# A trunk kernel whose weight sum of gate and up is formed by VectorE instead of an accumulating load

## The chip, the cores and the metric

The kernel runs on one core of one Trainium2 chip. The metric is the device time of one execution in microseconds (us). TensorE multiplies matrices, VectorE and ScalarE work on tiles element by element, GpSimd and SyncE (SP) mainly issue transfers (DMAs). Each engine takes its own instructions in order; semaphores hold an instruction back until what it needs is there.

## What is computed

A trunk of two layers on x of 512 tokens by 1024, in float32. In each layer, a SwiGLU block comes before and after a mixing block:

```python
def swiglu(h, w_gate, w_up, w_down):
    return (jax.nn.silu(h @ w_gate) * (h @ w_up)) @ w_down

for l in range(DEPTH):
    x = x + 0.5 * swiglu(rms_norm(x, ffn1_norm[l]), ffn1_wg[l], ffn1_wu[l], ffn1_wd[l])
    ...
    x = x + 0.5 * swiglu(rms_norm(x, ffn2_norm[l]), ffn2_wg[l], ffn2_wu[l], ffn2_wd[l])
return rms_norm(x, final_norm)
```

The gate and up weights `wg` and `wu` are 1024 by 2816, so there are four such blocks (FFNs) with 11 column blocks of 256. The change concerns only how a sum of raw weights is formed for the products with `wg` and `wu`.

## The kernel before, in words

*Precision.* TensorE multiplies in a reduced format. Each operand is therefore split into a high part (a cast on ScalarE) and a low part (raw minus high, on VectorE), both at line 228, and three products are taken: high x high, high x low and low x high. The weights' parts are the tiles `wh` and `wl`, three buffers each; those of the activations are called by their form, for example `fb11h` and `fb11l`.

*Stages.* An FFN walks over its column blocks in the order of `INNER` (line 33; the last FFN uses `LAST`): one plain block, then `("w", b)` stages for b = 1, 3, 5, 7, 9, each of which handles a pair of gate and up for two column blocks. A `w` stage uses a scheme with seven products in place of eight. Its seven weight forms, in the order of `FORMS` (line 38), are built from raw quarters of `wg` and `wu`. With g0, g1 for the upper and lower half of the 1024 rows of `wg` and u0, u1 for `wu`:

- a11 = g0
- a12 = g1
- s2 = g0 + u0 + u1
- s3 = u0 + g0
- s1 = u0 + u1
- a22 = u1
- s4 = a12 + s2

Each form comes in two halves, h0 and h1, of two 128-row chunks each, so a stage has fourteen halves. For each, `stream` (line 831) runs 12 matmuls of 128 x 512. `winograd2` (line 985) runs the stage on TensorE by `CHAINS` (line 69): a11 into x, a12 into w, s2 into x, s3 into y, s1 into x, a22 into y, s4 into x. For each half it first calls `take_split`, which makes the raw tiles and splits two halves ahead, and it then combines the accumulators x, y, w on VectorE and ScalarE (lines 1011 to 1029): L1014 adds for the gates, L1022 and L1025 subtract, L1026 and L1029 multiply with the gates.

*Raw tiles and queues.* `seven` (line 375) enters ten raw units per stage in this order: a11, s1, a12, s3, a22, two halves each. Units s1 and s3 name two sources each. `need_raw` (line 212) gives a unit one of eight raw buffers and issues its plain load on SP's queue (`load`, line 207, L210). A second source is added by an accumulating load on GpSimd's queue (L223), which waits until the first load has landed. `need_split` (line 236) makes the forms: before s2 is split, VectorE adds s1 to a11 in place (L269), and after s3 VectorE adds that sum to a12 in place (L291), which is s4. A raw buffer is free again when the last split of its tile is done; the next unit in line then takes it.

*Order.* A scheduler sets the order of instructions on each engine at build time, by dependencies; it may move a VectorE instruction well ahead of its place in the text. Once built, the order is fixed.

The first layer's first FFN is called with `near=True` and treats b = 1 and b = 3 specially; the stages b = 9 go over into the next kind of stage (`share`, line 846), which reads `wd` and is not touched.

Of the kernel before, what the change touches and what calls it, by code (L numbers as in the profile page):

```python
# [75 lines left out]
def trunk_kernel(  # L76
# [23 lines left out]
    nc = tc.nc  # L100
# [92 lines left out]
    units = []  # L193
# [6 lines left out]
    def add_unit(*unit):  # L200
        units.append(unit)
        return len(units) - 1
# [24 lines left out]
    def split(hi, lo, raw, eng=nc.vector):  # L227
        return nc.scalar.copy(hi, raw), eng.tensor_sub(lo, raw, f32(hi))  # L228

    def split_far(hi, lo, raw):  # L230

        nc.scalar.activation(lo, raw, AF.Copy, scale=-1.0)
        nc.scalar.copy(hi, raw)
        return nc.gpsimd.dma_start(out=f32(lo), in_=raw, accum_op=ALU.add)

    def need_split(g):
        while state["split"] <= min(g, len(order) - 1):
            n = state["split"]
            u, what = order[n]
            far = what == "far"  # L240
            if what in (None, "far"):
                need_raw(u if far else max(u, min(u + LOAD_AHEAD, state["hold"] or len(units))))
                raw = raw_of.pop(u)
            elif isinstance(what, tuple) and what[0] == "end":

                _, what, h = what
                at = {"a11": 2, "s2": 2, "s3": 3, "s1": 3, "a12": 4, "a22": 5, "s4": 5}[what]
                need_raw(u + 3 * at + h + LOAD_AHEAD)
                raws = {name: u + 3 * i + h for i, name in enumerate(END_LOADS)}
                if what == "s2":  # L250
                    with tc.issue_after(state["rest"]):
                        nc.vector.tensor_add(raw_of[raws["a11"]], raw_of[raws["a11"]], raw_of[raws["s1"]])
                raw = raw_of[raws["a11" if what in ("s2", "s4") else what]]
            elif isinstance(what, tuple):

                what, h, how = what
                far = how == "far"
                last = {"a11": 0, "a12": 4, "s2": 2, "s3": 6, "s1": 2, "a22": 8, "s4": 4}[what]
                need_raw(u + h if far else u + max(last, 4) + h + LOAD_AHEAD)
                a11, s1, a12, s3, a22 = (raw_of.get(u + 2 * i + h) for i in range(5))  # L260
                if what == "s2":

                    late = state["late"] if h else None
                    if not state["late"] and how == "share":
                        late = state["rest"]
                    if how == "behind":
                        late = state["mark"]
                    with tc.issue_after(late) if late else nullcontext():
                        nc.vector.tensor_add(a11, a11, s1)  # L269
                raw = {"a11": a11, "a12": a12, "s2": a11, "s3": s3, "s1": s1, "a22": a22, "s4": a12}[what]  # L270
            shape = list(raw.shape)
            hi = wpool.tile(shape, F32R, tag="wh", bufs=3, name=f"wh_{n}")
            lo = wpool.tile(shape, F32R, tag="wl", bufs=3, name=f"wl_{n}")
            if far:
                sent = split_far(hi, lo, raw)
            else:
                state["cast"], state["rest"] = (i.ins for i in split(hi, lo, raw))
                if isinstance(order[n][1], tuple) and order[n][1][2] == "mark":
                    state["mark"] = state["rest"]
            if isinstance(order[n][1], tuple) and order[n][1][0] == "end":  # L280
                if what == "a12":
                    nc.gpsimd.dma_start(out=raw_of[raws["a11"]], in_=raw, accum_op=ALU.add)
                if what in ("s3", "s1", "a12", "a22"):
                    del raw_of[raws[what]]
                if what == "s4":
                    del raw_of[raws["a11"]]
            elif isinstance(order[n][1], tuple):
                if what == "s3" and how == "share":
                    nc.gpsimd.dma_start(out=a12, in_=a11, accum_op=ALU.add)
                elif what == "s3":  # L290
                    nc.vector.tensor_add(a12, a12, a11)  # L291
                done = {"s3": (0, 3), "s1": (1,), "a22": (4,), "s4": (2,)}.get(what, ())
                for i in done:
                    del raw_of[u + 2 * i + h]
            split_of[n] = (hi, lo)
            state["split"] += 1
            if far:

                with tc.issue_after(sent.ins):
                    need_raw(u + LOAD_AHEAD + (4 + h if isinstance(order[n][1], tuple) else 0))  # L300
# [26 lines left out]
    def abreast(kc):  # L327

        return max(1, KC // kc) if kc in (2, 4) else 1
# [34 lines left out]
    def plan():  # L364
        def cols(src, k0, kc, n, how=None, last=False):
            wide = abreast(kc)
            for b in halves_of(n, wide, last):
                order.append((add_unit((src, k0, kc, b * P, wide * P)), how))

        def plain(wg, wu, b):  # L370
            for w in (wg, wu):
                for j in range(2):
                    order.append((add_unit((w, 0, KC, (2 * b + j) * P, P)), None))

        def seven(at, how):


            u = len(units)
            for what in (((0, 0),), ((1, 0), (1, 1)), ((0, 1),), ((1, 0), (0, 0)), ((1, 1),)):
                for h in range(2):  # L380
                    add_unit(*(at(o, j, h) for o, j in what))
            order.extend((u, (what, h, how(what, h))) for what in FORMS for h in range(2))

        def ffn(wg, wu, wd, stages, near=False):
            for what, b in stages:
                how = "far" if b == (0,) and not near else None
                if what == "p":
                    plain(wg, wu, b)
                if what == "w":
                    seven(  # L390
                        lambda o, j, h: ((wg, wu)[o], KC // 2 * j + 2 * h, 2, 2 * b * P, S),
                        lambda what, h: "far"
                        if (b, what, h) == (1, "a11", 0)
                        else {("a12", 0): "mark", ("s2", 1): "behind"}.get((what, h))
                        if near and b == 3
                        else None,
                    )
                if what == "s":
                    seven(
                        lambda o, j, h: (wd, 2 * b + KC // 2 * j + 2 * h, 2, o * S, S),  # L400
                        lambda what, h: "share",
                    )
                if what == "d":
                    cols(wd, 2 * b[0], 2 * len(b), KC, how, len(b) == 2)
                    if len(b) == 2:
                        closing.append(len(units) - 1)
                if what == "e":
                    u = len(units)
                    roomy.update(range(u, u + 3))
                    for form_ in END_LOADS:  # L410
                        ojs = {"s1": ((1, 0), (1, 1)), "s3": ((1, 0), (0, 0))}
                        for i in range(3):
                            add_unit(
                                *(
                                    (wd, 2 * b + (KC + 2 * j if i == 2 else KC // 2 * j + 2 * i), 2, o * S, S)
                                    for o, j in ojs.get(form_, ((0, int(form_ == "a12")) if form_ != "a22" else (1, 1),))
                                )
                            )
                    order.extend((u, ("end", what, i)) for what in END_FORMS for i in range(3))

        for l in range(DEPTH):
            ffn(ffn1_wg[l], ffn1_wu[l], ffn1_wd[l], INNER, l == 0)
            for c in MIX_COLS:
                for j in range(2):
                    order.append((add_unit((w_in[l], 0, KC, (2 * c + j) * P, P)), None))
            seven(
                lambda o, j, h: (w_out[l], KC // 2 * j + 2 * h, 2, o * S, S),
                lambda what, h: "share",
            )
            ffn(ffn2_wg[l], ffn2_wu[l], ffn2_wd[l], INNER if l + 1 < DEPTH else LAST)  # L430
# [1349 lines left out]
```

## Time and profile before

| | |
|---|---|
| median of 3 runs | 1625.92 us (1625.47 to 1626.92) |
| the profiled execution's own time | 1628.27 us |
| its span, first to last instruction | 1626.5 us |
| TensorE busy | 1616.2 us |
| VectorE busy | 1367.3 us |
| ScalarE busy | 1177.8 us |
| GpSimd busy | 223.5 us |
| mean data rate of the DMAs | 196 GB/s |
| accumulating loads of `wg` on GpSimd's queue | 40, of 512 KB each |

In the profile PE is TensorE's matmuls, PEld its weight loads, DVE is VectorE, ACT ScalarE, POOL GpSimd, and SPq the queue of SyncE. L228 is line 228. A row of a timeline gives start and duration in us from the span's start, engine, line, operation, output tile <- input tiles, the shape, how many instructions were merged into the row, and in brackets the idle time of the engine before it with what ended it. A DMA's row shows its issue; its landing, when the data has arrived, is given apart.

### The profile page before, as it was taken

To read this page: it belongs to the slowest core of one execution; us is meant where nothing else is said; L and a number is where in the kernel's file an instruction comes from. 1 tells how busy PE (TensorE), PEld (TensorE's weight loads), DVE (VectorE), ACT (ScalarE), POOL (GpSimd) and SP (SyncE) were. 2 spreads that over 40 slices of the span, in tenths; PEclk is the share of its full clock that TensorE was granted. 3 is DMA by queue.
4 is the path that set the end of the run, shared out by engine and by line. 5 is a ranking of instruction groups with operands and counts; after the bars stand their busy time and mean duration, and the time that the engine had idled before them with its cause. 6 is when DMAs were issued, how large, how long until landed. Compare 5 with 4: busy or idle time off the path is not lost.

```text
span 1626.5 us, 21177 instructions
## 1 busy us (share of the span) xinstructions
PE 1616.2 (99%) x7571; PEld 1349.5 (83%) x7571; DVE 1367.3 (84%) x1780; ACT 1177.8 (72%) x1511; POOL 223.5 (14%) x199
## 2 busy tenths in 40 slices
PE   9999999999999999999999999999999999999998
PEld 7888888888898878888888888888888988888887
DVE  7978797988899877797999777989788998677997
ACT  6677777857766577778865777788586767878665
POOL 1211111001211111111011111110012111111121
PEclk9999999999999999999999999999999999999999
DMA  9999999912597798999867899999136978999992
GB/s 269 213 231 213 215 215 236 242 58 77 145 230 170 177 218 214 214 218 246 224 147 186 215 216 221 211 245 224 48 91 154 235 149 215 228 221 226 231 264 71
DMA packets 307182, 318.12 MB, mean 196 GB/s; under 512 B 125628, under 2 KB 188676, under 8 KB 307076
## 3 DMA queue, kind: packets, MB, share of 16 engines
q1 hardware_dynamic: 265412, 230.90, 49.6%
q0 software_dynamic: 41200, 85.47, 30.7%
q8 instruction: 59, 0.97, 0.2%
q14 instruction: 47, 0.39, 0.1%
q10 hardware_dynamic: 464, 0.40, 0.1%
HBM read 264.29 MB, written 2.10 MB: 164 GB/s over the span
## 4 chain that ended last, share of the span: by engine, by line
PE 96%; DMA 2%; DVE 1%; ACT 0%; issue 0%; SPq 0%; POOL 0%; DVEq 0%; POOLq 0%
PE x L837 26%; PE y L837 13%; PE x_s L837 9%; PE acc L318 7%; PE acc L319 7%; PE acc L321 7%; PE w L837 7%; PE y_s L837 4%; PE x_m L822 3%; PE w_s L837 3%; PE y_m L822 1%; DMA raw<-in_ffn_wu_dram 1%; PE y_e L837 1%; PE x_e L837 1%; PE acc L699 1%; PE w_m L822 1%
## 5 line engine op out<-in xcount | busy, mean ns | idle before, releaser
L228 DVE TENSOR_TENSOR wl<-raw,wh 128x1024 fp32r<-128x1024 f32 (+1 forms) x494 | 598.7, 1219 | 171.4 <-ACT wh L228 170.3
L228 ACT CAST wh<-raw 128x1024 fp32r<-128x1024 f32 (+1 forms) x494 | 513.8, 1043 | 304.7 <-PE x L837 92.9
L318 PE MATMUL acc<-xh,wh 128*128 128x512 f32 x392 | 153.3, 393 | 0.5 <-ACT wh L228 0.5
L319 PE MATMUL acc<-xl,wh 128*128 128x512 f32 x392 | 153.1, 391 | 0.0
L321 PE MATMUL acc<-xh,wl 128*128 128x512 f32 x384 | 149.6, 390 | 0.0
L223 POOL DMA_DIRECT2D raw<-in_ffn_wu_dram x40 | 50.3, 1268 | 384.3 <-DMA raw<-in_ffn_wu_dram 182.6
L318 PEld LDWEIGHTS acc<-xh,wh 128*128 128x128 f32 x392 | 73.8, 188 | 15.1 <-ACT wh L228 0.6
L319 PEld LDWEIGHTS acc<-xl,wh 128*128 128x128 f32 x392 | 73.7, 188 | 14.4
L321 PEld LDWEIGHTS acc<-xh,wl 128*128 128x128 f32 x384 | 72.1, 188 | 15.2
L223 POOL DMA_DIRECT2D raw<-in_ffn_wg_dram x40 | 49.4, 1248 | 201.8 <-DMA raw<-in_ffn_wu_dram 92.0
L223 POOL DMA_DIRECT2D raw<-in_ffn_wd_dram x34 | 41.1, 1216 | 248.8 <-DMA raw<-in_ffn_wd_dram 86.8
L269 DVE TENSOR_TENSOR raw<-raw,raw 128x1024 f32<-128x1024 f32 x58 | 70.5, 1219 | 5.5 <-issue 3.1
L837 PE MATMUL w<-wl,fb21h 128*128 128x512 f32 x160 | 62.4, 390 | 1.5 <-DVE wl L228 1.5
L1101 ACT COPY raw_a<-turned 128x1024 uint16<-128x1024 uint16 x48 | 63.4, 1355 | 0.0
L837 PE MATMUL x<-wl,fb11h 128*128 128x512 f32 x160 | 62.4, 390 | 0.0
L837 PE MATMUL x<-wl,ft1h 128*128 128x512 f32 x160 | 62.4, 390 | 0.0
L837 PE MATMUL w<-wh,fb21h 128*128 128x512 f32 x160 | 62.3, 390 | 0.0
L837 PE MATMUL y<-wh,ft3h 128*128 128x512 f32 x160 | 62.3, 390 | 0.0
L837 PE MATMUL x<-wh,fb11l 128*128 128x512 f32 x160 | 62.3, 389 | 0.0
L837 PE MATMUL x<-wh,ft2l 128*128 128x512 f32 x160 | 62.3, 389 | 0.0
L837 PE MATMUL x<-wh,ft1h 128*128 128x512 f32 x160 | 62.3, 389 | 0.0
L837 PE MATMUL x<-wh,ft1l 128*128 128x512 f32 x160 | 62.3, 389 | 0.0
(517 smaller groups left out, 4542.3 us busy)
## 6 DMA issues: line engine op xcount, KB each, us to landing
raw<-in_ffn_wu_dram SPq DMA_DIRECT2D x127, 512.0 KB, 5.6
raw<-in_ffn_wd_dram SPq DMA_DIRECT2D x105, 512.0 KB, 6.2
raw<-in_ffn_wg_dram SPq DMA_DIRECT2D x86, 512.0 KB, 5.3
raw<-in_ffn_wu_dram POOLq DMA_DIRECT2D x40, 512.0 KB, 9.2
raw<-in_ffn_wg_dram POOLq DMA_DIRECT2D x40, 512.0 KB, 6.3
raw<-in_w_in_dram SPq DMA_DIRECT2D x36, 512.0 KB, 4.0
raw<-in_ffn_wd_dram POOLq DMA_DIRECT2D x34, 512.0 KB, 9.3
raw<-raw POOLq DMA_DIRECT2D x21, 512.0 KB, 7.4
```

The lines of the kernel that those rows point to most:

```text
L223: nc.gpsimd.dma_start(out=r, in_=rows_of(*more), accum_op=ALU.add)
L228: return nc.scalar.copy(hi, raw), eng.tensor_sub(lo, raw, f32(hi))
L269: nc.vector.tensor_add(a11, a11, s1)
L318: nc.tensor.matmul(acc, hi[:, k, :], rhs[k][0], start=k == first, stop=False)
L319: nc.tensor.matmul(acc, hi[:, k, :], rhs[k][1], start=False, stop=False)
L321: nc.tensor.matmul(acc, lo[:, k, :], rhs[k][0], start=False, stop=k == last)
L699: nc.tensor.matmul(opening[n], (lo if part == "w" else hi)[:, k, :], xl if part == "x" else xh, start=n not in begun, stop=k == KC - 1 and ...
L822: nc.tensor.matmul(accs[c // 2][:, c % 2, :], w[:, k, cols], x_[:, 2 * h + k, :], start=start and c % 2 == 0 and h + k + i == 0, stop=h + ...
L837: nc.tensor.matmul(accs[u], x_[:, 2 * h + k, tok], w[:, k, :], start=start and h + k + i == 0, stop=h + k == 2 and i == 2, skip_group_chec ...
L1101: nc.scalar.copy(words(raws[self.b][:, c, :]), self.to[:, :, c, :])
```

## The change

In most `w` stages the raw unit s3 is loaded with one source, `wu`, in place of two. The second summand, the gate's first quarter, already lies in the tile of a11, and VectorE adds it to s3's tile: `nc.vector.tensor_add(s3, s3, a11)`, 128 x 1024, entered in the text when the half of a12 has been split. It reads a11 before L269 overwrites it. The new argument `here` selects the stages: b = 1, 3, 5, 7 of each FFN, without b = 1 of the first layer's first FFN; that is 15 stages with two halves each. The `share` stages and the last stages keep both sources.

```diff
@@ -285,6 +285,8 @@
                 if what == "s4":
                     del raw_of[raws["a11"]]
             elif isinstance(order[n][1], tuple):
+                if what == "a12" and len(units[u + 6 + h]) == 1:
+                    nc.vector.tensor_add(s3, s3, a11)
                 if what == "s3" and how == "share":
                     nc.gpsimd.dma_start(out=a12, in_=a11, accum_op=ALU.add)
                 elif what == "s3":
@@ -372,11 +374,12 @@
                 for j in range(2):
                     order.append((add_unit((w, 0, KC, (2 * b + j) * P, P)), None))
 
-        def seven(at, how):
+        def seven(at, how, here=False):
 
 
             u = len(units)
-            for what in (((0, 0),), ((1, 0), (1, 1)), ((0, 1),), ((1, 0), (0, 0)), ((1, 1),)):
+            s3 = ((1, 0),) if here else ((1, 0), (0, 0))
+            for what in (((0, 0),), ((1, 0), (1, 1)), ((0, 1),), s3, ((1, 1),)):
                 for h in range(2):
                     add_unit(*(at(o, j, h) for o, j in what))
             order.extend((u, (what, h, how(what, h))) for what in FORMS for h in range(2))
@@ -394,6 +397,7 @@
                         else {("a12", 0): "mark", ("s2", 1): "behind"}.get((what, h))
                         if near and b == 3
                         else None,
+                        here=b < 9 and (b > 1 or not near),
                     )
                 if what == "s":
                     seven(
```

## The prediction

> **What bounds the kernel now.** I began with the page's first part, engines with busy time, share of the span and instructions:
>
> ```profile
> PE 1616.2 (99%) x7571; PEld 1349.5 (83%) x7571; DVE 1367.3 (84%) x1780; ACT 1177.8 (72%) x1511; POOL 223.5 (14%) x199
> ```
>
> TensorE is idle for 1626.5 - 1616.2 = 10.3 us in all. So anything that makes TensorE wait is added to the time nearly whole, and a relief elsewhere can give back a few microseconds at most. Busy time by stretches says where the idle time lies and how full an undisturbed stage is (a pair of gate and up is one stage of 38.08 us: fourteen halves of 12 matmuls, 2.72 us each):
>
> ```profile
> core 0: us, PE busy (x) PEld busy (x) DVE busy (x) ACT busy (x) POOL busy (x), PEclk, DMA share, GB/s
> 926.27:964.35 38.08, 38.08 (x170) 31.54 (x169) 27.69 (x30) 28.09 (x33) 4.85 (x4) 1.00 0.95 222
> ...
> 568.40:609.00 40.60, 39.06 (x173) 32.01 (x172) 31.88 (x33) 28.35 (x33) 6.01 (x5) 1.00 0.93 217
> ```
>
> In the middle of the run TensorE stops once only, 1.5 us in the second row. In a stage VectorE has 27.69 us of work for 38.08 us, so the two added sums fit in by total. Totals don't decide this change, though: VectorE takes its instructions in order, and what counts is what stands behind a waiting one. So I read its timeline at one stage boundary (start, duration, line, operation, how many, idle time before):
>
> ```profile
> 920.15 1.41 DVE L1025 TENSOR_TENSOR u<-y,u 128x512 f32<-128x512 f32 x2
> 921.48 1.28 DVE L1026 TENSOR_TENSOR u<-u,gate 128x512 f32<-128x512 f32 x2
> 922.68 1.22 DVE L228 TENSOR_TENSOR wl<-raw,wh 128x1024 fp32r<-128x1024 f32 x1
> 923.93 1.23 DVE L269 TENSOR_TENSOR raw<-raw,raw 128x1024 f32<-128x1024 f32 x1
> 925.08 1.22 DVE L228 TENSOR_TENSOR wl<-raw,wh 128x1024 fp32r<-128x1024 f32 x1
> 926.21 0.68 DVE L1029 TENSOR_TENSOR p<-p,gate 128x512 f32<-128x512 f32 x1
> 926.82 1.22 DVE L269 TENSOR_TENSOR raw<-raw,raw 128x1024 f32<-128x1024 f32 x1
> ...
> 928.80 1.23 DVE L228 TENSOR_TENSOR wl<-raw,wh 128x1024 fp32r<-128x1024 f32 x1 [0.17 <-ACT wh L228]
> ```
>
> The split at 922.68 is a11 h0 of the next stage, 925.08 is a11 h1, 928.80 is a12 h0 (the L269 add of s2 overwrites a11, so it stands behind a11's split). Steps from start to start: 1.15 us for 128x1024, 0.60 for 128x512. When TensorE needs a11 h0 is seen in the chain of waits (start, length) and in the weight load of that half:
>
> ```profile
> 920.83 10.88 PE x L837 x48
> ...
> L837 PEld LDWEIGHTS x<-wl,fb11h x1: 187/187/187, 926.3 to 926.3; 128*128 128x128 f32 x1
> ```
>
> 48 matmuls are s4 and a11; a11 begins at P = 920.83 + 5.44 = 926.27, and its low part must stand in wl by P + 0.08. It does at 923.90.
>
> **The change, part by part.** In 15 stages the load of s3 brings wu alone. Two accumulating loads per stage go, 30 in all, and 30 additions of 128x1024 come on VectorE. GpSimd loses 2 issues per stage; at 14% busy that is worth nothing.
>
> *What the removed loads were worth.* They start when s3 has landed, 926.73 below, and s3's split comes at 936.44, the earliest use; nothing on TensorE waited for them, so removing them gives nothing there.
>
> *The additions' own time.* The same operation exists:
>
> ```profile
> L269 DVE TENSOR_TENSOR raw<-raw,raw 128x1024 f32<-128x1024 f32 x58 | 70.5, 1219 | 5.5 <-issue 3.1
> ```
>
> 30 x 1.22 = 36.6 us, 2.44 in a stage. VectorE is idle for 38.08 - 27.69 = 10.4 us of a stage, mostly in its later part, so the additions are hidden if they may lie there; at the boundary above it has next to no idle time, and there they cost 1.15 each.
>
> *Where they stand and what they wait for.* In the changed kernel as built, the order on VectorE at this boundary is: u of y (first), **sum h0**, u times gate (first), u of y (second), split of a11 h0, u times gate (second), split of a11 h1, p, **sum h1**, p, split of a12 h0, L269, split of a12 h1, L269, split of s2 h0, L291 twice, split of s2 h1. The sum h0 needs s3's load, which until now was wanted only at 936.44, and a11's split stands behind it. SP's and GpSimd's timelines show that load, and SP's line alone how long it takes:
>
> ```profile
> 917.54 3.09 SPq L210 DMA_DIRECT2D raw<-in_ffn_wu_dram  x2
> DMA to landing us min/median/max: 8.6/8.6/8.6
> ...
> 912.28 2.47 POOL L223 DMA_DIRECT2D raw<-in_ffn_wu_dram  x2 [21.65 <-DVE wl L228]
> 926.73 2.45 POOL L223 DMA_DIRECT2D raw<-in_ffn_wg_dram  x2 [11.97 <-DVE wl L228]
> ```
>
> Issued at 917.54, landed at 926.16 (GpSimd's row begins 0.57 later, which reads the landing in the other stages). The issue can't come sooner: it waits for the slot that s4 h0's split frees, and that follows TensorE. What flies beside it, s1's two accumulates from 912.28 and a12's load, stays.
>
> Stall in this stage: landing 926.16 + 0.10 to wake; sum 1.15; two of 0.60; split 1.22; 0.05 to TensorE: wl stands at 929.88 instead of 926.35. That is 3.53 us, or (landing - P) + 3.64. The next halves then come in time, with TensorE 3.53 later: a12 h0 at 935.1 where 935.3 would do, s2 h1 at 943.2 for 943.5, s3 later with room; VectorE has caught up by the end of the stage, and s4 h0's split, and so the next s3 load, is again set by TensorE. So the stall recurs in each such stage.
>
> Seven stages have this order (the third in the first FFN, the third and fourth in the other three). The first and last, and two other kinds beside them:
>
> ```profile
> 77.82 10.88 PE x L837 x48
> 115.90 10.88 PE x L837 x48
> 153.98 10.88 PE x L837 x48
> 1364.39 10.88 PE x L837 x48
> 1440.55 10.88 PE x L837 x48
> ...
> 84.88 2.44 POOL L223 DMA_DIRECT2D raw<-in_ffn_wg_dram  x2 [10.14 <-DMA raw<-in_ffn_wu_dram]
> 121.66 2.48 POOL L223 DMA_DIRECT2D raw<-in_ffn_wg_dram  x2 [10.51 <-DVE wl L228]
> 158.75 2.47 POOL L223 DMA_DIRECT2D raw<-in_ffn_wg_dram  x2 [10.51 <-DVE raw L269]
> 1371.61 1.21 POOL L223 DMA_DIRECT2D raw<-in_ffn_wg_dram  x1 [11.17 <-DMA raw<-in_ffn_wu_dram]
> 1445.29 2.44 POOL L223 DMA_DIRECT2D raw<-in_ffn_wg_dram  x2 [9.87 <-DVE raw L269]
> ```
>
> First: landing 121.09, P 121.34: 3.4 us. Last: 1444.72 and 1445.99: 2.4. With the five between (2.4, 2.0, 3.5, 3.3, 3.0 from the same views) the seven make 20.0 us.
>
> In the five other stages after the first of an FFN the sum h0 stands behind a11 h0's split, and the split of a11 h1, due 2.72 later, waits for it. Where s3 lands after P it still bites: P 83.26, landing 84.31: a11 h1 0.75 late, and with sum h1 in its chain a12 h0 1.55 late. P 1369.83, landing 1371.04: 1.7. P 159.42, landing 158.18: a11 h1 comes in time, but there both L269 stand between the splits of a12 h1 and s2 h0, with bias work before them, and s2 h0 is 1.0 late. One (P 888.19, landing 0.5 earlier) keeps 0.1 us in hand and costs 0. The fifth is where TensorE stops already:
>
> ```profile
> 555.60 12.70 DMA raw<-in_ffn_wu_dram
> 571.41 5.28 PE w L837 x22
> ...
> 568.68 1.20 POOL L223 DMA_DIRECT2D raw<-in_ffn_wg_dram  x1 [2.76 <-DMA raw<-in_ffn_wu_dram]
> ```
>
> There L269 of h1 waits for s1's accumulate until 568.30 and a12's split stands behind it; the matmul at 571.41 is 2.1 late. The new order puts a12's split ahead of that L269 but behind sum h1, whose load lands there at 568.1 by GpSimd's row: 2.1 again, no change. Together 4.3.
>
> In the first stage of three FFNs s3's first half is there early, but VectorE is dense:
>
> ```profile
> 528.27 2.35 DVE L228 TENSOR_TENSOR wl<-raw,wh 128x1024 fp32r<-128x1024 f32 x2
> ...
> 531.67 2.35 DVE L269 TENSOR_TENSOR raw<-raw,raw 128x1024 f32<-128x1024 f32 x2
> 533.95 1.21 DVE L228 TENSOR_TENSOR ft1l<-hf,ft1h 128x1024 fp32r<-128x1024 f32 x1
> 535.08 2.35 DVE L228 TENSOR_TENSOR wl<-raw,wh 128x1024 fp32r<-128x1024 f32 x2
> ...
> 536.47 5.44 PE x L837 x24
> ```
>
> Both sums stand ahead of s2 h0's split, which moves from 535.08-536.29 to 537.4-538.6. The new order on TensorE takes four more high-part matmuls first, so low is due at 536.47 + 4 x 0.23 + 0.08 = 537.5: 1.2 late, and some 0.2 more at s1 h0. 1.4 x 3 = 4.2.
>
> Sum: 20.0 + 4.3 + 4.2 = 28.5 us. The profiled execution took 1628.27 with its span of 1626.5, and the median of the runs shown is 2.35 below it, so I put the sum on the median: 1625.92 + 28.5 = **1654.4**.
>
> *Bounds.* The free term is s3's time to land. Below: the median of such loads,
>
> ```profile
> raw<-in_ffn_wu_dram SPq DMA_DIRECT2D x127, 512.0 KB, 5.6
> ```
>
> would leave 3.53 - 3.0 = 0.5 in each of the seven and nothing in the five; with the first stages hidden too, 1625.9 + 3.7 = 1629.6. Above: the load that landed at 1371.04 is the slowest plain load of an s3 with a quoted landing,
>
> ```profile
> DMA to landing us min/median/max: 10.0/10.0/10.0
> ```
>
> 1.5 more than 8.6 in 11 stages: 1671. I take the landings as measured, since what flies beside them stays.
>
> *The clock.* The stretch with the present stop has a granted clock of 1.00, and the run's mean is
>
> ```profile
> core 0: 1626.5 us, clock 0.999
> ```
>
> so a stop of 2.1 us lost no clock. [...]
>
> **The rivals.**
> 1. *The load lands in time.* With 30 accumulating loads fewer the s3 loads could come in at the 5.6 us median, or 3.6 us sooner than at 917.54; from there no stall is left in the seven, and if the first stages hide their sums the time is 1625.9, at most 1629. For: the DMA share is 0.95 in that stage. Against: the removed loads flew from 926.73 on, after the landing, so they never slowed it.
> 2. *Faster.* If sum h1's load near 568 came sooner, the 2.1 us stop would go: 1623.8, which is still within what counts as no change. More than that needs the opening and closing idle time, which the change doesn't touch.
> [...]
> 4. *Late all through.* a12 h0 and s2 h1 come with 0.2 and 0.3 us in hand; 0.5 us more at each of 12 stages gives 1660, inside the range.
>
> **How the numbers follow.** Forecast with its spread (2 and 4 included): 85%; clock: 8%; load in time: 6%; faster: 1%. Range 1636 to 1670: from two thirds of the sum's stalls missing to the 10 us landing. About 0.2% (3.3 us) is what a measurement of this kernel can tell from no change: faster 0.02, same 0.05, slower 0.93.
>
> **What would show it.** TensorE idle for 2 to 3.5 us at the start of the third and fourth stages, released by VectorE's L228 on wl, and VectorE idle just before the new sum, released by a DMA of wu, with s3's landing 7 to 8.6 us after its issue. TensorE busy unchanged, GpSimd 30 issues fewer, VectorE 36.6 us busier. Wrong if VectorE doesn't wait before the sums, if the stops come at other forms than a11, or if the granted clock falls below 0.99.

## The result and the profile after

The changed kernel takes 1667.72 us (median of 6 runs, 1664.21 to 1675.49); the kernel before, run beside it, takes 1626.54 us (6 runs, 1625.47 to 1630.01). The ratio is 1.0259, 95% interval 1.0239 to 1.0278: 41 us slower. The profiled execution took 1664.34 us.

The busy line of the page and its line of GpSimd's queue (packets, MB, share of 16 engines), after:

```profile
PE 1628.5 (98%) x7571; PEld 1351.8 (81%) x7571; DVE 1396.4 (84%) x1810; ACT 1176.8 (71%) x1511; POOL 187.3 (11%) x169
...
q0 software_dynamic: 33040, 69.74, 24.3%
```

The list of cores, after (span, mean granted clock):

```profile
core 0: 1662.6 us, clock 0.996
```

The counts are what the change says: 30 more instructions on VectorE, 30 fewer on GpSimd, the same 7571 matmuls. TensorE is idle for 1662.6 - 1628.5 = 34.1 us, where it was 10.3. But its *busy* time grew too, by 12.3 us for the same matmuls, and the mean granted clock went from 0.999 to 0.996. Some of the loss is thus not waiting. Not all of the 12.3 is clock either: matmuls' ends are modelled, and a stop of 2.25 us from start to start (945.97 to 948.22) shows as 1.86 of idle time.

The page's groups of the new sum and of the low-part matmuls of a11, after (busy us, mean ns | idle time of the engine just before them, and what ended most of it):

```profile
L841 PE MATMUL x<-wl,fb11h 128*128 128x512 f32 x160 | 65.7, 411 | 19.2 <-DVE wl L228 19.1
...
L289 DVE TENSOR_TENSOR raw<-raw,raw 128x1024 f32<-128x1024 f32 x30 | 36.7, 1222 | 49.3 <-issue 29.0
```

The waits of TensorE, after (total us, times, longest):

```profile
PE x L841 <- DVE wl L228: 20.2, 11, 4.5
PE w L841 <- DVE wl L228: 2.0, 4, 0.6
```

And those of VectorE:

```profile
DVE raw L289 <- issue: 29.0, 6, 6.8
DVE raw L289 <- DMA raw<-in_ffn_wu_dram: 20.2, 6, 4.4
```

L289 is the new sum. Its work is 36.7 us, as worked out, but VectorE stood idle 49.3 us in front of it: 20.2 us are put down to the load of wu, 29.0 us to "issue", which means that the profile shows no releaser. Nearly all of TensorE's new waiting is for `wl`. (Before, the same group of matmuls had a mean of 390 ns and no idle time.)

One of the seven stages on VectorE's timeline, after (start, duration, idle before with its releaser):

```profile
606.50 1.22 DVE L228 TENSOR_TENSOR wl<-raw,wh 128x1024 fp32r<-128x1024 f32 x1 [1.49 <-ACT wh L228]
607.65 0.68 DVE L1029 TENSOR_TENSOR u<-y,u 128x512 f32<-128x512 f32 x1
613.27 1.22 DVE L289 TENSOR_TENSOR raw<-raw,raw 128x1024 f32<-128x1024 f32 x1 [4.94 <-issue]
614.42 0.68 DVE L1030 TENSOR_TENSOR u<-u,gate 128x512 f32<-128x512 f32 x1
615.02 0.68 DVE L1029 TENSOR_TENSOR u<-y,u 128x512 f32<-128x512 f32 x1
615.62 1.22 DVE L228 TENSOR_TENSOR wl<-raw,wh 128x1024 fp32r<-128x1024 f32 x1
```

The same moment on TensorE's timeline:

```profile
613.83 0.39 PE L841 MATMUL x<-wh,fb11l 128*128 128x512 f32 x1
616.89 0.50 PE L841 MATMUL x<-wl,fb11h 128*128 128x512 f32 x1 [2.67 <-DVE wl L228]
...
618.10 0.63 PE L841 MATMUL x<-wh,fb11h 128*128 128x512 f32 x1
618.53 0.63 PE L841 MATMUL x<-wh,fb11l 128*128 128x512 f32 x1
```

This is the chain of the prediction, instruction for instruction: VectorE has nothing it may do from 608.33 until the sum starts at 613.27, then come 1.15 + 2 x 0.60 + 1.22, and TensorE starts at 616.89, which is 3.62 after the sum's start. When did s3 land? SP's line for the window in which both halves' loads are issued, the first at 605.04:

```profile
L210 SPq DMA_DIRECT2D raw<-in_ffn_wu_dram x2: 368/368/368, 605.0 to 607.8; - x2
...
DMA to landing us min/median/max: 6.7/7.4/8.2
```

The half issued first took 8.2 us and landed at 613.2, right before the sum starts. So what the profile calls "issue" is this load as well. In four of the other five waits given so, the sum also starts within 0.1 us of the landing of its load of wu, in the fifth 0.4 us after it.

The second thing to read is the spacing of the matmuls behind the stop. From 618.10 they start 0.43 us apart; elsewhere it is 0.23. Busy time by stretches shows the clock there, after:

```profile
core 0: us, PE busy (x) PEld busy (x) DVE busy (x) ACT busy (x) POOL busy (x), PEclk, DMA share, GB/s
127.00:135.00 8.00, 7.89 (x35) 6.53 (x36) 8.00 (x10) 3.13 (x5) 0.00 (x0) 1.00 0.00 0
616.80:620.40 3.60, 3.51 (x10) 2.79 (x11) 3.60 (x6) 0.00 (x0) 0.00 (x0) 0.62 0.00 0
616.50:625.00 8.50, 8.11 (x28) 6.50 (x29) 8.50 (x10) 2.97 (x4) 0.00 (x0) 0.80 0.00 0
947.50:956.00 8.50, 7.79 (x27) 6.25 (x28) 8.50 (x10) 3.52 (x5) 0.00 (x0) 0.80 0.01 2
989.00:998.00 9.00, 7.63 (x33) 6.30 (x34) 9.00 (x11) 4.08 (x6) 0.00 (x0) 1.00 0.00 0
1440.00:1448.00 8.00, 7.39 (x26) 6.01 (x27) 8.00 (x10) 2.46 (x3) 0.00 (x0) 0.79 0.00 0
```

After the stops that end at 616.89, 948.22 and 1440.61 the granted clock is 0.8 over some 8 us, so 0.2 x 8.5 = 1.7 us are lost behind each; after those that end at 127.11 and 990.37 it is 1.00. The chain of waits has the same difference (start and length of the matmuls behind two of the stops):

```profile
948.22 6.91 PE x L841 x22
...
990.37 5.32 PE x L841 x22
```

The first took 1.6 us longer than the second for the same 22 matmuls.

### The profile page after: what moved, and what is told of

Read it like the earlier page. It is cut to its first block, busy times and chain, and to the rows that moved or that the text cites. A ratio compares the mean times of both kernels' runs of the same rounds, so it can differ in the third digit from the quotient of the medians.

```text
span 1662.6 us, 21137 instructions
## 1 busy us (share of the span) xinstructions
PE 1628.5 (98%) x7571; PEld 1351.8 (81%) x7571; DVE 1396.4 (84%) x1810; ACT 1176.8 (71%) x1511; POOL 187.3 (11%) x169
## 4 chain that ended last, share of the span: by engine, by line
PE 84%; DVE 7%; DMA 4%; issue 3%; ACT 2%; SPq 0%; DVEq 0%; ACTq 0%
PE x L841 21%; PE y L841 10%; PE x_s L841 9%; PE acc L320 7%; PE acc L321 7%; PE acc L323 7%; PE w L841 6%; PE y_s L841 4%; DVE wl L228 3%; DMA raw<-in_ffn_wu_dram 3%; PE x_m L826 3%; PE w_s L841 3%; PE y_m L826 1%; ACT wh L228 1%; PE y_e L841 1%
## 5 line engine op out<-in xcount | busy, mean ns | idle before, releaser
L289 DVE TENSOR_TENSOR raw<-raw,raw 128x1024 f32<-128x1024 f32 x30 | 36.7, 1222 | 49.3 <-issue 29.0
L269 DVE TENSOR_TENSOR raw<-raw,raw 128x1024 f32<-128x1024 f32 x58 | 70.4, 1219 | 0.1
L841 PE MATMUL x<-wh,fb11h 128*128 128x512 f32 x160 | 64.1, 401 | 0.0
L841 PE MATMUL y<-wh,ft4h 128*128 128x512 f32 x160 | 62.5, 390 | 1.0 <-ACT wh L228 1.0
L841 PE MATMUL x<-wl,ft2h 128*128 128x512 f32 x160 | 62.0, 391 | 1.1 <-DVE wl L228 1.1
L841 PE MATMUL y<-wl,ft3h 128*128 128x512 f32 x160 | 62.0, 390 | 0.3 <-DVE wl L228 0.3
```

The source lines that it names most:

```text
L289: nc.vector.tensor_add(s3, s3, a11)
L841: nc.tensor.matmul(accs[u], x_[:, 2 * h + k, tok], w[:, k, :], start=start and h + k + i == 0, stop=h + k == 2 and i == 2, skip_group_chec ...
```

## The experiments

The theory was the prediction's: the 41 us come from sums that wait, ahead of a split, for s3's load, and from the clock that falls after some of the stops. The rivals: the added work itself (36.7 us on an engine that is dense at the stage boundary), and other places of loss.

**again**: the changed kernel once more, beside the next three.

> The changed kernel once more, as the yardstick on this chip. All theories: 1664 to 1676 us, seven stops of TensorE of 2 to 5 us at the first half of a11, a granted clock of 0.991 to 0.996 (before: 0.999).

Measured 1667.44 us (1665.16 to 1673.6), ratio 1.0259 (1.0237 to 1.0281); a second set of runs gives the same result.

**sum_behind**: the same sums, held behind the split that stands before them in the text.

```diff
-                    nc.vector.tensor_add(s3, s3, a11)
+                    with tc.issue_after(state["rest"]):
+                        nc.vector.tensor_add(s3, s3, a11)
...
-                    nc.vector.tensor_add(a12, a12, a11)
+                    with tc.issue_after(state["rest"]):
+                        nc.vector.tensor_add(a12, a12, a11)
```

> The same 30 sums on VectorE and the same loads, but the sum is held behind the split of a12's half, and the sum for s4 behind the split of s3's half. Theory of the wait (the sum stands ahead of a11's split and waits there for s3's load): by then the load has landed, the twelve later stages lose nothing, the three first stages some 1.4 us each: 1628 to 1633 us, granted clock 0.998 or more. Rival, the added work itself (36.6 us of VectorE): the work is all still there, so 1650 us or more.

Measured 1630.5 us (1630.34 to 1631.38), ratio 1.0026 (1.0015 to 1.0036). The sum's group:

```profile
L290 DVE TENSOR_TENSOR raw<-raw,raw 128x1024 f32<-128x1024 f32 x30 | 36.6, 1220 | 0.0
```

Thirty sums of the same length with no idle time before them, a mean granted clock of 0.999, and 37 of the 41 us are gone. VectorE does the same work in both, so the rival of the added work falls. Comparing the starts of TensorE's stages with those of before, twelve stages lose nothing, and the first stages of three FFNs lose 2.16, 0.89 and 0.48 us.

**sum_narrow**: the sum cut to an eighth of its columns, so that seven eighths of the sum for s3 are left out.

```diff
-                    nc.vector.tensor_add(s3, s3, a11)
+                    nc.vector.tensor_add(s3[:, :, :64], s3[:, :, :64], a11[:, :, :64])
```

> The sum keeps its place and its wait but covers 64 of the 512 columns, so it leaves out seven eighths of u0 + g0 in s3; some 0.3 us in place of 1.22. Theory of the wait: the stops stay, each about 0.95 us shorter, the first stages lose nothing: 1640 to 1652 us, VectorE still idle 3 to 6 us before the sum. Rival, the added work: nearly all of it is gone, 1626 to 1630 us.

Measured 1671.44 us (1670.85 to 1673.44), ratio 1.028 (1.0263 to 1.0297). The expectation missed: the scheduler placed the cheaper sum ahead of a11 h0's split in nine stages in place of seven, and it still waits there:

```profile
DVE raw L289 <- issue: 46.2, 9, 6.6
DVE raw L289 <- DMA raw<-in_ffn_wu_dram: 17.5, 7, 6.0
```

It says nothing clean about the sum's length, but with an eighth of the work no time came back: the wait goes with the place.

**filled**: the changed kernel, with matmuls of zeros for TensorE to run while it waits.

```diff
+                    if fill and u + k == 0 and i == 2:
+                        into = psum("aux", [P, S], "fill")
...
+                                last = nc.tensor.matmul(
+                                    into, zero[:, :P], zero, start=True, stop=True
+                                ).ins
```

> Ten matmuls of zeros (2.2 us) are put on TensorE between the high and the low parts of the first half of a11 in the seven stages that stop longest; nothing else is changed. If the stops also cost clock: the granted clock stays at 0.998 or more, and the time falls by the three slow spells of some 1.7 us or more, to 1655 to 1661 us, with less scatter than the changed kernel. If the clock does not matter: the time of the changed kernel, or up to 3 us above it, where a stop was shorter than the 2.2 us.

Measured 1677.58 us (1667.66 to 1682.8), ratio 1.0308 (1.0272 to 1.0345). A miss, and not a clean test: the longer stage on TensorE changed the order on VectorE as well, and each of the seven stages got a second stop at `w<-wl,fb21h` (1.69 us at 967.46).

**behind_from3**: sum_behind, with the first stage of each FFN given back its accumulating loads.

```diff
-                        here=b < 9 and (b > 1 or not near),
+                        here=1 < b < 9,
```

> The kernel of sum_behind, with the first stage of each FFN given back its accumulating loads (12 stages keep the VectorE sums, held behind). sum_behind lost 2.16 + 0.89 + 0.48 = 3.5 us in three first stages, nothing in the other 12, and the 2.1 us stop near 568 was gone. Theory (the added work is hidden wherever the sum doesn't stand ahead of a split; the first stages pay for it because VectorE is dense there): 1630.5 - 3.5 = 1627.0 or a little less, 1624 to 1627, no slower than before, and the stage near 568 still without its stop. Rival (the 3.5 us came from elsewhere, from the order that holding the sums gives): the time stays at 1629 to 1631.

Measured 1626.87 us (1626.34 to 1627.38, 11 runs), ratio 0.9999 (0.999 to 1.0008). So the first stages cost 1630.5 - 1626.87 = 3.6 us and the twelve others nothing that these runs can tell. This is the change without its loss, and it gains nothing either.

**before_s4_behind**: the kernel before, with the sum for s4 held behind s3's split and nothing else (the lower half of sum_behind's edit).

> The kernel before, with nothing of the change, and only the sum for s4 (L291 there) held behind s3's split as in sum_behind. Theory (near 568 it was the displaced order around the new sum that let a12's split go ahead of the waiting L269): the 2.1 us stop near 568 stays, time 1625 to 1628. Rival (holding the s4 sum alone removes it, so that gain of sum_behind has nothing to do with the change): stop gone, 1623 to 1625.

Measured 1626.38 us (1625.91 to 1628.31), ratio 0.9997 (0.9988 to 1.0006). Its trace has no stop near 568, so sum_behind's lack of that stop isn't owed to the change. That the held sum is what removes it, as the rival has it, isn't shown: the time lies above the rival's 1623 to 1625, and the median didn't move. The span, 1624.5, is also that of a run of the kernel before that took 1626.34 us, while the profiled execution of before took 1628.27 with a span of 1626.5. That most runs of before are without this stop is likely, but no trace of them shows it.

**pinned** and **pinned_fill**: the clock again, now with VectorE's order tied down, without and with the zero matmuls.

```diff
+                    late = late or state["rest"]
...
+                    with tc.issue_after(state["rest"]):
+                        nc.vector.tensor_add(a12, a12, a11)
```

> The changed kernel, new sums where its scheduler puts them, but L269 and the sum for s4 tied behind the split before them, so that VectorE's order no longer depends on TensorE's times. It is the partner of pinned_fill, which has instruction for instruction the same order on VectorE. Both theories: stops of 2 to 5 us at a11 in the seven stages as in the changed kernel, 1660 to 1675, granted clock 0.991 to 0.996, in stretches of 8.5 us after some of the stops 0.80.

> As pinned, with ten matmuls of zeros (0.23 us each, 2.3 us) into an unused bank between the high and the low part of a11 h0 in the seven stages, so that TensorE works while it waits for wl. Its output is the reference's. Theory (about three of the stops cost 1.7 us of granted clock each on top of their length): no stretch under 0.95 after the seven stops, and 3 to 6 us less than pinned; the fill itself costs only where a stop is under 2.3 us, at most 1 us in all. Rival (the lower clock rows are a sign and not a cost, or the clock falls for another reason than the stop): same time as pinned or up to 3 us more, or clock rows under 0.9 in spite of the fill.

Measured 1660.34 us (1658.63 to 1663.62; ratio 1.0206, 1.0191 to 1.022) and 1672.18 (1670.45 to 1673.93; 1.0276, 1.0262 to 1.029). Both expectations missed (pinned's time lies just inside its range, but without the stops and the clock that were expected), for one reason: the tied order took the long stops away and spread the loss over many short ones, the longest 1.69 us. TensorE's waits for wl in pinned (total us, times, longest):

```profile
PE x L843 <- DVE wl L228: 4.9, 8, 1.1
PE w L843 <- DVE wl L228: 4.8, 9, 1.2
```

With no long stop to fill, the fill was pure cost, 12 us for 70 matmuls of 0.23. One thing follows even so: with stops of at most 1.69 us the mean granted clock stays at 0.999 while the kernel loses 34 us.

**ahead_alone**, **ahead_fill**, **ahead_early**: three kernels built on behind_from3. The first puts the sum h0 ahead of a11 h0's split in the seven stages, by order and not by the scheduler's choice:

```diff
+            elif isinstance(what, str) and isinstance(order[n][1], tuple) and order[n][1][2] == "early":
+                early.add(u)
+                ahead = nc.vector.tensor_add(s3, s3, a11)
+                cast = nc.scalar.copy(hi, raw)
+                with tc.issue_after(ahead.ins):
+                    rest = nc.vector.tensor_sub(lo, raw, f32(hi))
```

> behind_from3 with one difference: in the seven stages of the prediction's main term (third stage of the first FFN, third and fourth of the other three) sum h0 is put ahead of a11 h0's split on VectorE; all other sums stay held behind. Theory (a11 h0's split waits behind the sum for s3's load, so each of the seven stages stops as worked out: 3.4, 2.4, 2.0, 3.5, 3.3, 3.0, 2.4 = 20.0 us): 1626.9 + 20.0 = 1647, plus about 1.7 us for each stop after which the granted clock falls, at most 1657; TensorE's stops at x<-wl,fb11h in just these stages. Rival (the place of this one sum matters little, the loss comes from the density of VectorE's work, which is the same in both): 1626 to 1632.

The second is the first with the zero matmuls of filled, with every other engine's order as it was. The third is the first, without zero matmuls, with s3 loaded before a12 instead of after it; there the sum is also tied behind the split before it, which keeps VectorE's order:

```diff
-            for what in (((0, 0),), ((1, 0), (1, 1)), ((0, 1),), s3, ((1, 1),)):
+            mid = (((1, 0),), ((0, 1),)) if here else (((0, 1),), ((1, 0), (0, 0)))
...
+            for what in (((0, 0),), ((1, 0), (1, 1)), *mid, ((1, 1),)):
```

> ahead_alone with ten matmuls of zeros into an unused bank between the high and the low part of a11 h0 in the seven stages (2.3 us each), with the same order on every other engine. Its output is the reference's. Theory (the clock term is a cost of its own): if n of the stops of ahead_alone show 0.8 for the 8.5 us after them, this kernel is without them and 1.7 x n us faster, less what the fill costs where a stop is under 2.3 us (up to 2 us in all); if ahead_alone shows no such stretch, it is 0 to 2 us slower. Rival (the lower clock has nothing to do with TensorE's idling): stretches of 0.8 after the same stops in spite of the fill.

> ahead_alone with the load of s3 put ahead of that of a12 in the order of loads, for the twelve stages with the VectorE sum; the same instructions in the same order on VectorE. s3 is then issued two places earlier and a12 takes its old place, where it must land by 5.4 us after a11 begins. Theory (the price is the wait for s3's landing): the stops at a11 h0 are gone or under 0.8 us each, 1626 to 1632, the clock 0.999. Rival (the sum's place costs by its 1.2 us of work ahead of the split, or the loads as such collide): 1640 or more. A second rival (the wait only moves, to a12's split, which now waits for the late load): stops at w<-wl,fb21h or later, 1632 to 1645.

| kernel | median us | ratio to before, interval | clock of the profiled run |
|---|---|---|---|
| behind_from3 | 1626.87 | 0.9999 (0.999 to 1.0008) | 1.000 |
| ahead_alone | 1657.23 | 1.0189 (1.0163 to 1.0215) | 0.994 |
| ahead_fill | 1649.24 | 1.0138 (1.0121 to 1.0154) | 0.999 |
| ahead_early | 1627.89 | 1.0012 (1.0003 to 1.0022) | 0.999 |

One sum per stage in seven stages, placed three splits earlier, costs 30 us. ahead_alone's median lies just above the upper bound that was expected. Its waits on TensorE:

```profile
PE x L852 <- DVE wl L281: 23.5, 7, 5.2
```

And the stretches behind five of its seven stops (columns as above):

```profile
609.80:618.30 8.50, 8.45 (x28) 6.78 (x29) 8.29 (x9) 2.79 (x4) 0.00 (x0) 0.73 0.01 2
653.00:661.50 8.50, 8.33 (x37) 6.90 (x38) 8.47 (x10) 4.84 (x6) 0.00 (x0) 1.00 0.00 0
...
982.20:990.70 8.50, 8.43 (x30) 6.81 (x31) 8.47 (x10) 3.32 (x5) 0.00 (x0) 0.80 0.00 0
1430.60:1439.10 8.50, 8.48 (x31) 6.92 (x32) 8.46 (x9) 3.57 (x5) 0.00 (x0) 0.82 0.00 0
1474.50:1483.00 8.50, 8.41 (x30) 6.89 (x31) 8.47 (x10) 3.32 (x5) 0.00 (x0) 0.80 0.00 0
```

From the last matmul before to the first after, the stops are 2.62, 5.57, 3.16, 2.68, 4.22, 3.39 and 4.57 us; the clock falls after the second and the last three. The stretches lose (0.27 + 0.20 + 0.18 + 0.20) x 8.5 = 7.2 us. With TensorE kept busy, three of the same places, ahead_fill:

```profile
603.50:620.00 16.50, 15.87 (x70) 11.96 (x70) 16.33 (x18) 11.44 (x14) 0.00 (x0) 1.00 0.19 49
974.00:990.00 16.00, 15.91 (x70) 11.99 (x70) 15.97 (x18) 11.49 (x14) 0.00 (x0) 1.00 0.24 62
1462.00:1480.00 18.00, 16.13 (x71) 12.21 (x71) 16.36 (x18) 11.69 (x15) 0.00 (x0) 1.00 0.18 49
```

No stretch is below 1.00, and the kernel is 1657.23 - 1649.24 = 8.0 us faster *with* 70 more matmuls. Lost clock is a term of its own. (Not all of the difference is clock: the two profiled executions lie 8.9 us apart, of which the stretches explain 7.2, and the seven loads of s3 took 59.5 us to land in sum where they took 61.8.) What is left, 1649.24 - 1626.87 = 22.4 us, is the waiting, where 20.0 was worked out.

ahead_early has VectorE's instructions in the same order as ahead_alone. What is left of TensorE's waits for `wl`:

```profile
PE x L856 <- DVE wl L228: 0.2, 1, 0.2
```

The stage on VectorE's timeline, ahead_early:

```profile
595.34 1.23 DVE L228 TENSOR_TENSOR wl<-raw,wh 128x1024 fp32r<-128x1024 f32 x1 [1.49 <-ACT wh L228]
596.48 0.68 DVE L1044 TENSOR_TENSOR u<-y,u 128x512 f32<-128x512 f32 x1
597.08 1.22 DVE L280 TENSOR_TENSOR raw<-raw,raw 128x1024 f32<-128x1024 f32 x1
...
599.41 1.21 DVE L283 TENSOR_TENSOR wl<-raw,wh 128x1024 fp32r<-128x1024 f32 x1
```

The sum stands ahead of the split and doesn't wait. Its load is issued at 588.43 and lands 4.4 us later, while a12's, issued at 593.87 in s3's old place, takes 10.2 us; it is wanted later and nobody waits for it. So the price was the wait for the landing of s3, not the sum's place by itself and not its 1.2 us.

## Why the prediction was right, and what it mis-sized

*The mechanism.* Sum h0 ahead of a11 h0's split, VectorE idle until s3 lands, TensorE stopped at a11: shown by the timelines, by sum_behind (no wait, 1630.5) and by ahead_early (load early, 1627.89). That the removed loads were worth nothing is shown by behind_from3: 24 of them gone, 1626.87. The prediction's P, read from the chain, lies 0.16 us after a11's first matmul in TensorE's rows (926.11 for 926.27); no term of the sum changes by it, since the time by which wl is needed was read from the weight load.

*The seven stages, 20.0 us.* In the profiled execution their starts, set against those of before, show 3.91, 4.60, 1.99, 3.79, 2.49, 6.26 and 2.15, together 25.2, of which the three spells of clock are 5.1; 20.1 us of waiting are left. Single stages differ more than the sum (the sixth lost 4.7 us of waiting where 3.0 was worked out, as s3 took 10.0 us to land; the fourth 2.1 for 3.5), so part of the agreement is chance: with the forced order it was 22.4.

*The five later stages, 4.3 us.* Measured 1.16, 1.59 and 1.49 where 1.55, 1.0 and 1.7 were worked out, and 1.95 where the stage with 0.1 us in hand was taken as free: that hand was too small to count on. In the stage that stopped already the 2.1 us were replaced by 1.5. Since the forecast was set on the median, and most runs of before seem to lack that stop, 1.5 counts as missing there.

*The first stages, 4.2 us.* 2.05, 1.17 and 0.37, together 3.6; the two medians with and without them gave 3.6 too.

*The step that failed is the clock*, costed at nothing in the sum and left to a chance of 8%: "a stop of 2.1 us lost no clock" was read as a sign for stops of 2 to 3.5 us. In the profiled execution three stops cost 5.1 us, and its clock says the same: (0.999 - 0.996) x 1662.6 = 5.0. The six runs have 0.991 to 0.996, on the middle 0.994, and so some 0.005 x 1668 = 8 us in the median run. Behind a stop that cost clock about 8 matmuls started some 0.43 us apart in place of 0.23 (from 618.10, and from 948.79 at a clock of 0.50), 1.7 us by the stretches.

The rest of the 37.8 us between the profiled execution and the median of before: 28.5 forecast, 5.1 clock, 1.5 and 1.9 in the five later stages, 1.3 at the opening (0.1 in the trace of again, so not of the change), and -0.6 in the first ones. The 41 us of the medians hold more of the clock than this one run.

Which stops cost clock did not go by their length alone. The 3.41 us from the first slow matmul behind one stop, and as long a stretch behind another, after (columns as above):

```profile
948.79:952.20 3.41, 3.41 (x10) 2.64 (x9) 3.41 (x5) 0.20 (x1) 0.00 (x0) 0.50 0.02 5
...
989.75:993.16 3.41, 2.79 (x12) 2.29 (x13) 3.41 (x5) 0.86 (x2) 0.00 (x0) 1.00 0.00 0
```

The first lies behind a stop of 2.25 us (945.97 to 948.22), with TensorE at work for over 10 us before it: (1 - 0.50) x 3.41 = 1.7 us, the same estimate as from 0.2 x 8.5. The second holds the end of a stop of 2.54 us (to 990.37) and what follows it, at full clock. Nor did 3.20 us (to 127.11) cost clock, nor 2.24 (1480.04 to 1482.28, then 1.00 from 1482.20 to 1490.70); in ahead_alone the stop of 3.39 us did and that of 3.16 didn't. What made the difference isn't shown. The kernel before has a single stop of this kind, near 570, at 1.00 from 568.40 to 577.00, so it could not tell what other stops would do.

Of the signs named in advance, all came in kind but two, and not all in size: TensorE's idle time at the seven stops was 1.65 to 4.53 us for 2 to 3.5, s3 landed after 6.8 to 10.0 us for 7 to 8.6, and six of the twelve waits before the sum stand under "issue". The two: TensorE's busy time was not unchanged, and VectorE's grew by 29.1 us and not by 36.6, in part since neighbours overlap (1.22 us long, 1.15 from start to start). The clock stayed above the 0.99 that would have made the forecast wrong (0.991 at the lowest), which was too wide a bound to see 8 us by.

The rivals: "the load lands in time" falls (6.8 to 10.0 us from issue to landing in the seven stages of the changed kernel, 10.7 once in ahead_alone); "faster" falls; of "late all through" there is little, 2.0 us of waits at a12 in all (the row of w), where it let each of 12 stages lose 0.5.

## What to carry to other kernels

Replacing a transfer by an instruction on an in-order engine moves the moment at which the other operand must be there: from the first use of the result to the place of that instruction in the queue (here 1657.23 us with seven sums ahead of the split, 1626.87 with all of them behind it, 1627.89 with the load early). So ask first what the new instruction waits for and what stands behind it; its own time is the smaller question, and either an order (behind the urgent split) or an earlier load takes the price away. Where a change makes TensorE stop, weigh the clock behind the stop as a term of its own: here some 1.7 us behind three of the seven stops at a11 h0 in the changed kernel, and a clock of 0.73 to 0.82 over 8.5 us behind four of seven in ahead_alone, while in pinned, with no stop above 1.69 us, the mean clock stayed at 0.999. Length alone did not tell which stops would cost it.

## What the runs showed that was not expected

- A stop of 2.25 us was followed by a granted clock of 0.50 over 3.41 us (948.79 to 952.20), one of 3.20 us by 1.00 over 8 us (127.00 to 135.00).
- 70 matmuls of zeros in TensorE's waiting time made a kernel 8.0 us faster, with a mean granted clock of 0.999 in place of 0.994; in pinned_fill, where there was no long wait to fill, they cost 12 us.
- Landing went with the moment of issue and not with the tile in the stage that was read: in ahead_early s3 takes 4.4 us in the earlier place and a12 10.2 us in the later one, where s3 had taken 10.7 in ahead_alone.
